# One condition per expert above 32 tokens, a later block of 64 rows, and a branch hint for PE in a mixture-of-experts kernel

## The chip, the cores and the metric

The kernel runs on one core of a Trainium2 chip. The metric is the device time of one execution in microseconds (us); lower is better. The engines are named as in the profile: PE (TensorE, matrix products and transposes; PEld its loads of stationary operands), DVE (VectorE), ACT (ScalarE), POOL (GpSimd), SP (SyncE, which here issues transfers). A q behind a name (PEq, PEldq, SPq) is that engine's sequencer or its DMA queue.

## The reference

One decoder layer in float32 on 512 tokens of width 1024: attention heads and recurrent heads, a projection and a layer norm, cross-attention and a layer norm, and a hierarchical mixture of experts with a last layer norm. The change touches only the experts:

```python
g_prob = softmax(xt @ w_group + b_group)            # 4 groups, the best one is taken
top_p, top_i = top_k(softmax(logits of the group), 2)   # 2 of its 8 experts
...
def run_block(xblk, e):
    hid = silu(xblk @ w_gate[e]) * (xblk @ w_up[e])     # 1024 -> 512
    return hid @ w_down[e]                              # 512 -> 1024
...
y = yb * slot_w
out = segment_sum(y, slot_tok)
```

512 tokens with two experts each give 1024 rows for 32 experts. For these inputs the experts 0 to 31 get 41, 41, 19, 5, 15, 74, 64, 9, 0, 4, 14, 1, 21, 11, 55, 28, 10, 92, 53, 14, 14, 133, 30, 162, 2, 19, 34, 6, 17, 11, 4 and 21 rows. Ten have more than 32 (0, 1, 5, 6, 14, 17, 18, 21, 23, 26), four of these more than 64 (5, 17, 21, 23).

## The kernel before

The experts are taken in order by a Python loop, so each has its own code. Expert e's first 64 rows stand in one half of a tile `xT` (two experts share one, turned by `turn_pair`), its weights in six tiles of 1 MB (`wg`, `wu`, `wd`, two each) in a ring of 20 places. SP fills the ring: `pump(2)` and `pump(4)` (line L815) issue the next two and four tiles of the list at their place in SP's program, and each issue waits until its place is free.

`step(now, last, M)` is one expert's work on PE: gate and up of this expert, and in between the transposes (`turn`, L1154) and the product with `wd` (`down`) of the expert before. Every `mm` is line L75. It exists twice, in two arms of a condition on n, the number of thresholds (32, 64, 192, 320, 448) that the expert's count exceeds: `If(n > 0)` at L1260 takes 64 rows, its Else 32 rows. Behind it `later_blocks` (L1198) has a condition of its own, `If(n > 1)`: `block128` takes up to 128 further rows, fetched into `xo` ahead of time, through transposes (L1122), gate into `psg`, up into `psu`, transposes (L1186) and `psy`; a loop inside `If(n > 2)` (L1201, L1202) repeats it. `send` scatters the rows of a pair of experts, `fetch` gathers rows; both are on POOL.

The order on PE, DVE, ACT and POOL is as written; each engine runs the conditions itself, with its own register loaded by `number(e)` (L1211). Order within the loop: `number`, `fetch`, every second time `turn_pair` and `fetch_pair`, the condition of `step`, `send`, `pump(2)`, the condition of `later_blocks`, `pump(4)`.

Of the kernel before, what the change touches and what calls it, by code (L numbers as in the profile page):

```python
# [964 lines left out]
def moe(ctx, tc, A, out, x2, x2d, env):  # L965
# [78 lines left out]
    steps = iota("steps", [5], [[P, 5]], 0, base=-64)  # L1044
    V.tensor_scalar(steps, steps, 32.0, None, op0=OP.max)
    nb = gp.tile([1, NE, 5], F32, name="nb")
    V.tensor_tensor(nb, cnt[0:1].unsqueeze(2).to_broadcast([1, NE, 5]), steps[0:1].unsqueeze(1).to_broadcast([1, NE, 5]), OP.is_gt)
# [49 lines left out]
    def bank(name, tag):  # L1097
        return banks.tile([P, 512], F32, name=name, tag=tag)
# [25 lines left out]

    class Expert:


        def __init__(self, e):
            self.e, self.c, self.r = e, e // 2, slice(e % 2 * 64, e % 2 * 64 + 64)
            self.x = xT[self.c]  # L1130
            if e % 2 == 0:
                Ys[self.c] = ms.tile([P, D], F32, name="Y", bufs=2)

        def gate_up(self, M, steps):

            e = self.e
            if steps[0] == 0:
                self.ps = bank("psgu", f"g{e % 2}")
            n = P // M // 2
            w = 512 // n  # L1140
            for k in steps:
                for q in range(2 * n):
                    mm(self.ps[q * M:q * M + M, 0:w], self.x[:, k, self.r.start:self.r.start + M],
                       W[e, "ug"[q // n], k // 4][:, k % 4, q % n * w:(q % n + 1) * w], k == 0, k == KD - 1)
            if steps[-1] == KD - 1:
                for q in range(n):
                    h = self.hs[0:M, q * w:(q + 1) * w]
                    SC.activation(h, self.ps[64 + q * M:64 + q * M + M, 0:w], AF.Silu)  # L1148
                    V.tensor_tensor(h, h, self.ps[q * M:q * M + M, 0:w], OP.mult)  # L1149

        def turn(self):
            pt = bank("psht", "h")
            for c in range(4):
                PE.transpose(pt[:, c * 64:(c + 1) * 64], self.hs[:, c // 2 * 256 + c % 2:(c // 2 + 1) * 256:2], ident[0:64, 0:64])  # L1154
            V.tensor_copy(self.hT, pt[:, 0:256])  # L1155

        def down(self):
            e = self.e
            ps = bank("psy", f"y{e % 2}")
            for c in range(4):  # L1160
                for q in range(2):
                    mm(ps[q * 64:q * 64 + 64, :], self.hT[:, c * 64:(c + 1) * 64],
                       W[e, "d", c // 2][:, c % 2, q * 512:q * 512 + 512], c == 0, c == 3)
            for q in range(2):
                SC.copy(Ys[self.c][self.r, q * 512:q * 512 + 512], ps[q * 64:q * 64 + 64, :])  # L1165

        def send(self):
            if self.e % 2:
                scatter(Ys[self.c], first_y[:, self.c:self.c + 1])

# [25 lines left out]
    def later_blocks(e, n, rows):  # L1196

        with tc.If(n > 1):  # L1198
            tiles = [ms.tile([P] + c, F32, name=t) for t, c in (("ox", [KD, P]), ("oh", [512]), ("oT", [512]))]
            block128(e, rows, tiles, later_y[:, 0, e:e + 1])  # L1200
            with tc.If(n > 2):  # L1201
                with tc.For_i(2, n) as c:  # L1202
                    c = nc.s_assert_within(c - 1, 1, 3, skip_runtime_bounds_check_because=FITS)
                    idx = ms.tile([P, 2], I32, name="oi")
                    for m, t in enumerate((later_x, later_y)):
                        V.tensor_copy(idx[:, m:m + 1], t[:, bass.ds(c, 1), e:e + 1].rearrange("p c e -> p (c e)"))
                    fetch(rows, idx[:, 0:1])
                    block128(e, rows, tiles, idx[:, 1:2])

    def number(e):  # L1210
        return nc.values_load(regs[0:1, e:e + 1], min_val=0, max_val=5, skip_runtime_bounds_check_because=FITS)  # L1211
# [26 lines left out]

    with tc.manual_schedule(engines={mybir.EngineType.PE, mybir.EngineType.DVE, mybir.EngineType.Activation, mybir.EngineType.Pool}):
# [7 lines left out]
        Expert.hs, Expert.hT = hs, hT  # L1247
# [3 lines left out]
        for e in range(NE):  # L1251
# [8 lines left out]
            with tc.If(n > 0) as many:  # L1260
                step(now, last, 64)
            with many.Else():
                step(now, last, 32)
            if last:
                last.send()
                pump(2)
            else:
                later_slots(marks)
                fetch(rows, later_x[:, 0, 0:1])
                cG.close()  # L1270
                env["cT"].close()
                env["more"](ctx, "ringC", RING_C)
            later_blocks(e, n, rows)
# [88 lines left out]
```

## Time and profile before

| | |
|---|---|
| three runs, median (lowest to highest) | 1177.45 us (1168.74 to 1178.84) |
| the profiled execution | 1178.46 us |
| its span, mean granted clock of TensorE | 1176.7 us, 0.931 |
| PE, PEld, DVE, ACT, POOL busy | 991.0, 649.1, 404.1, 312.6, 279.7 us |

The time is the device time of an execution; the span runs from the first to the last instruction in the trace of the profiled one. Busy shares are means over stages with different limits: the experts begin at about 584 us, half way, and before them the layer's other parts run. A group's row in the profile names line, engine, operation and tiles; where a row shows idle time, the name behind the arrow is what ended it.

### The profile page before, as it was taken

How to read it: one execution, taken by the hardware profiler on the slowest of the kernel's cores; microseconds unless marked ns; L12 is line 12 of the kernel's file. 1: busy time of each engine (PE TensorE's matmuls, PEld its weight loads, DVE VectorE, ACT ScalarE, POOL GpSimd, SP SyncE). 2: the span in 40 equal slices, each digit the busy share in tenths (PEclk: the TensorE clock that was granted, in tenths of full speed). 3: DMA queues.
4: the chain of work that ended last, by engine and by line, in shares of the span. 5: the costliest groups of instructions: out<-in, count | busy, mean ns of one | idle time of the engine just before them, and what ended most of it. 6: DMA issues, size and time to landing. Idle time of an engine off the chain costs nothing. (4 is left out here: it accounts for less than half of the span.)

```text
span 1176.7 us, 16302 instructions
## 1 busy us (share of the span) xinstructions
PE 991.0 (84%) x6260; PEld 649.1 (55%) x6260; DVE 404.1 (34%) x865; ACT 312.6 (27%) x612; POOL 279.7 (24%) x210
## 2 busy tenths in 40 slices
PE   7999999989899999999477997777897887877860
PEld 6787798768688998889223433332332333433320
DVE  8528607656835514345611101111100111011117
ACT  4434423433633534421011101111110101011132
POOL 4431243115124672331211101121101101011112
PEclk9999999999999999999688998898998899998885
DMA  6730231011043452178669959999999949299934
GB/s 206 218 105 24 56 101 37 1 36 55 20 143 93 141 163 71 54 264 332 265 263 413 413 210 397 414 411 414 413 417 400 403 183 407 98 412 412 411 109 180
DMA packets 88618, 269.59 MB, mean 229 GB/s; under 512 B 16191, under 2 KB 57212, under 8 KB 63870
## 3 DMA queue, kind: packets, MB, share of 16 engines
q1 hardware_dynamic: 76926, 252.67, 56.0%
q0 software_dynamic: 10512, 11.04, 2.8%
q10 hardware_dynamic: 1008, 3.67, 0.8%
q8 instruction: 98, 1.61, 0.6%
q14 instruction: 74, 0.61, 0.1%
HBM read 279.91 MB, written 14.68 MB: 250 GB/s over the span
## 5 line engine op out<-in xcount | busy, mean ns | idle before, releaser
L75 PE MATMUL psgu<-wu,xT 128*32 128x256 f32 (+1 forms) x864 | 190.9, 504 | 56.1 <-issue 32.2
L148 POOL TENSOR_TENSOR hl<-raw,hl 128x1024 fp32r<-128x1024 f32 (+1 forms) x67 | 161.4, 2411 | 252.9 <-ACT hl L145 201.9
L75 PE MATMUL psgu<-wg,xT 128*32 128x256 f32 (+1 forms) x864 | 192.8, 504 | 8.7 <-issue 8.7
L75 PEld LDWEIGHTS psgu<-wu,xT 128*32 128x32 f32 (+1 forms) x864 | 66.3, 134 | 151.5 <-issue 119.9
L75 PE MATMUL psy<-wd,hT 128*64 128x512 f32 x512 | 118.4, 600 | 0.7 <-ACTq L1198 0.6
L145 ACT CAST hl<-raw 128x1024 fp32r<-128x1024 f32 (+1 forms) x68 | 70.3, 1040 | 92.0 <-PE psm L75 39.0
L1114 POOL DMA_INDIRECT xo<-x2d,later_x x32 | 32.1, 1004 | 202.8 <-ACTq L1198 55.6
L1155 DVE COPY hT<-psht 128x256 f32<-128x256 f32 x32 | 13.6, 424 | 191.0 <-PE psht L1154 186.2
L1148 ACT ACTIVATE hs<-psgu 32x256 f32<-32x256 f32 (+1 forms) x54 | 22.6, 418 | 208.8 <-PE psgu L75 196.9
L75 PEld LDWEIGHTS psy<-wd,hT 128*64 128x64 f32 x512 | 35.3, 138 | 72.0 <-issue 70.2
L1149 DVE TENSOR_TENSOR hs<-hs,psgu 32x256 f32<-32x256 f32 (+1 forms) x54 | 24.8, 460 | 145.0 <-ACT hs L1148 82.5
L1165 ACT COPY Y<-psy 64x512 f32<-64x512 f32 x64 | 37.1, 580 | 135.2 <-PE psy L75 132.4
L75 PEld LDWEIGHTS psgu<-wg,xT 128*32 128x32 f32 (+1 forms) x864 | 66.8, 134 | 8.7 <-issue 8.4
L75 PE MATMUL psm<-hl,XO 128*128 128x256 f32 x384 | 50.7, 287 | 1.4 <-DVE x L680 1.4
L1122 PE MATMUL psgt<-ident,xr 128*128 128x128 f32 x128 | 22.6, 323 | 33.5 <-PEq L1198 21.2
L75 PE MATMUL psm<-hl,mix 128*128 128x256 f32 x320 | 49.1, 291 | 0.6 <-DVE x L680 0.5
L1106 POOL DMA_INDIRECT yd<-Y,first_y x16 | 16.1, 1009 | 139.4 <-ACTq L1198 125.8
L75 PEld LDWEIGHTS psm<-hl,XO 128*128 128x128 f32 x384 | 47.3, 191 | 2.1 <-DVE x L680 1.8
L75 PE MATMUL psxq<-x1T,hl 128*128 128x512 f32 x192 | 46.7, 396 | 0.0
L75 PEld LDWEIGHTS psm<-hl,mix 128*128 128x128 f32 x320 | 43.5, 193 | 3.5 <-issue 1.3
L75 PE MATMUL psq<-xT,hl 128*128 128x512 f32 x192 | 45.2, 395 | 0.0
L1122 PEld LDWEIGHTS psgt<-ident,xr 128*128 128x128 f32 x128 | 18.5, 212 | 46.2 <-issue 28.9
(368 smaller groups left out, 1669.4 us busy)
## 6 DMA issues: line engine op xcount, KB each, us to landing
wg<-in_moe_w_gate_dram SPq DMA_DIRECT2D x64, 1024.0 KB
wu<-in_moe_w_up_dram SPq DMA_DIRECT2D x64, 1024.0 KB
wd<-in_moe_w_down_dram SPq DMA_DIRECT2D x64, 1024.0 KB
raw<-in_w_in_dram SPq DMA_DIRECT2D x22, 512.0 KB
raw<-in_w_out_dram SPq DMA_DIRECT2D x8, 512.0 KB
raw<-in_xa_wv_dram SPq DMA_DIRECT2D x8, 512.0 KB
raw<-in_xa_wk_dram SPq DMA_DIRECT2D x8, 512.0 KB
raw<-in_xa_wq_dram SPq DMA_DIRECT2D x8, 512.0 KB
```

Source lines behind the costliest of these rows:

```text
L75: PE.matmul(o, l, r, start=start, stop=stop, skip_group_check=True)
L145: cp = SC.copy(hl[:, 0], raw)
L148: (V if n - look < on_dve else PO).tensor_tensor(hl[:, 1], raw, f(hl[:, 0]), OP.subtract)
L1106: t = PO.indirect_dma_start(out=yd, out_offset=bass.IndirectOffsetOnAxis(ap=idx, axis=0), in_=Y, in_offset=None, bounds_check=2 * S - 1, o ...
L1114: PO.indirect_dma_start(out=rows, out_offset=None, in_=x2d, in_offset=bass.IndirectOffsetOnAxis(ap=idx, axis=0), bounds_check=S - 1, oob_i ...
L1122: PE.transpose(ps[:, k * P:(k + 1) * P], rows[:, a * 512 + k:(a + 1) * 512:4], ident)
L1148: SC.activation(h, self.ps[64 + q * M:64 + q * M + M, 0:w], AF.Silu)
L1149: V.tensor_tensor(h, h, self.ps[q * M:q * M + M, 0:w], OP.mult)
L1155: V.tensor_copy(self.hT, pt[:, 0:256])
L1165: SC.copy(Ys[self.c][self.r, q * 512:q * 512 + 512], ps[q * 64:q * 64 + 64, :])
```

## The change

The thresholds become 128, 32, 64, 192, 320 and 448. For every expert but the first there is one condition, `If(n > 0, label="more{e}")`. Its arm holds the 64-row `step` and, nested, the later blocks: `If(n > 1)`, in it `If(n > 2)` with `block128` and its loop (now `n > 3`), and in that one's Else the new `block64`, for up to 64 further rows in the form of the 64-row arm. Its Else is the 32-row `step`. `send`, `pump(2)` and `pump(4)` stand behind the condition. Both arms begin with `hint(e + 1)`: an instruction on PE that names the next expert's condition and says that its branch, to the Else, is likely taken.

```diff
-    steps = iota("steps", [5], [[P, 5]], 0, base=-64)
-    V.tensor_scalar(steps, steps, 32.0, None, op0=OP.max)
-    nb = gp.tile([1, NE, 5], F32, name="nb")
-    V.tensor_tensor(nb, cnt[0:1].unsqueeze(2).to_broadcast([1, NE, 5]), steps[0:1].unsqueeze(1).to_broadcast([1, NE, 5]), OP.is_gt)
+    steps = iota("steps", [6], [[P, 6]], 0, base=-192)
+    V.memset(steps[:, 0:1], 128.0)
+    V.memset(steps[:, 1:2], 32.0)
+    nb = gp.tile([1, NE, 6], F32, name="nb")
+    V.tensor_tensor(nb, cnt[0:1].unsqueeze(2).to_broadcast([1, NE, 6]), steps[0:1].unsqueeze(1).to_broadcast([1, NE, 6]), OP.is_gt)
...
+    def gate_up(ps, x, e, steps, M=64):
+
+        n = P // M // 2
+        w = 512 // n
+        for k in steps:
+            for q in range(2 * n):
+                mm(ps[q * M:q * M + M, 0:w], x[:, k, 0:M],
+                   W[e, "ug"[q // n], k // 4][:, k % 4, q % n * w:(q % n + 1) * w], k == 0, k == KD - 1)
...
+    def block64(e, rows, tiles, idx):
+
+        xe, hs, hT = tiles[0][:, :, 0:64], tiles[1][0:64], tiles[2][:, 0:256]
+        tags = "o", f"y{e % 2}"
+        for a in range(2):
+            ps = bank("psgt", tags[a])
+            for k in range(4):
+                PE.transpose(ps[:, k * 64:(k + 1) * 64], rows[0:64, a * 512 + k:(a + 1) * 512:4], ident[0:64, 0:64])
+            (SC.copy if a else V.tensor_copy)(xe[:, 4 * a:4 * a + 4, :], ps[:, 0:256].rearrange("p (k t) -> p k t", t=64))
+        ps = bank("psg", "o")
+        gate_up(ps, xe, e, range(KD))
+        hidden(ps, hs)
+        turn(hs, hT)
+        down(bank("psy", tags[1]), hT, e, rows[0:64])
+        scatter(rows, idx)
...
     def later_blocks(e, n, rows):
 
+        def tiles():
+            return [ms.tile([P] + c, F32, name=t) for t, c in (("ox", [KD, P]), ("oh", [512]), ("oT", [512]))]
+
         with tc.If(n > 1):
-            tiles = [ms.tile([P] + c, F32, name=t) for t, c in (("ox", [KD, P]), ("oh", [512]), ("oT", [512]))]
-            block128(e, rows, tiles, later_y[:, 0, e:e + 1])
-            with tc.If(n > 2):
-                with tc.For_i(2, n) as c:
-                    c = nc.s_assert_within(c - 1, 1, 3, skip_runtime_bounds_check_because=FITS)
-                    idx = ms.tile([P, 2], I32, name="oi")
-                    for m, t in enumerate((later_x, later_y)):
-                        V.tensor_copy(idx[:, m:m + 1], t[:, bass.ds(c, 1), e:e + 1].rearrange("p c e -> p (c e)"))
-                    fetch(rows, idx[:, 0:1])
-                    block128(e, rows, tiles, idx[:, 1:2])
+            with tc.If(n > 2) as more:
+                ts = tiles()
+                block128(e, rows, ts, later_y[:, 0, e:e + 1])
+                with tc.If(n > 3):
+                    with tc.For_i(3, n) as c:
+                        c = nc.s_assert_within(c - 2, 1, 3, skip_runtime_bounds_check_because=FITS)
+                        idx = ms.tile([P, 2], I32, name="oi")
+                        for m, t in enumerate((later_x, later_y)):
+                            V.tensor_copy(idx[:, m:m + 1], t[:, bass.ds(c, 1), e:e + 1].rearrange("p c e -> p (c e)"))
+                        fetch(rows, idx[:, 0:1])
+                        block128(e, rows, ts, idx[:, 1:2])
+            with more.Else():
+                block64(e, rows, tiles(), later_y[:, 0, e:e + 1])
...
+    def hint(e):
+        if e < NE:
+            tc.mark_branch_hint_location(f"more{e}", "LikelyTaken", engines=[mybir.EngineType.PE])
...
-            with tc.If(n > 0) as many:
-                step(now, last, 64)
-            with many.Else():
-                step(now, last, 32)
-            if last:
-                last.send()
-                pump(2)
-            else:
+            if e == 0:
+                with tc.If(n > 0) as many:
+                    step(now, last, 64)
+                with many.Else():
+                    step(now, last, 32)
                 later_slots(marks)
                 fetch(rows, later_x[:, 0, 0:1])
                 cG.close()
                 env["cT"].close()
                 env["more"](ctx, "ringC", RING_C)
-            later_blocks(e, n, rows)
+                hint(1)
+                later_blocks(e, n, rows)
+            else:
+                with tc.If(n > 0, label=f"more{e}") as many:
+                    hint(e + 1)
+                    step(now, last, 64)
+                    later_blocks(e, n, rows)
+                with many.Else():
+                    hint(e + 1)
+                    step(now, last, 32)
+                last.send()
+                pump(2)
             pump(4)
             last = now
 
```

The functions `gate_up`, `hidden`, `turn` and `down` hold what the methods of `Expert` held; `block64` uses them for `rows[0:64]`, with gate and up in one bank `psg`.

How the program stands on PE. Before, from the end of expert 1's 32-row arm to the loop behind its later block (names: `psy` is a product with `wd`, `xo` the later rows, `ox`, `oh` and `oT` the block's copies):

```order
L75 MATMUL psgu<-wg,xT 32x256 x2
L75 MATMUL psy<-wd,hT 64x512 x8
L1260 UNCONDITIONAL_BRANCH
L1198 COMPARE_AND_BRANCH
L1122 MATMUL psgt<-ident,xo 128x128 x8
L75 MATMUL psg<-wg,ox 128x512 x8
L75 MATMUL psu<-wu,ox 128x512 x8
L1186 MATMUL psht<-ident,oh 128x128 x4
L75 MATMUL psy<-wd,oT 128x512 x8
L1201 COMPARE_AND_BRANCH
L1202 COMPARE_AND_BRANCH
L1202 UNCONDITIONAL_BRANCH x2
```

The two arms of the step join here, and only then comes the condition of the later block. In the changed program, the end of expert 2's 64-row arm: both new conditions and the block of 128 follow it directly:

```order
L75 MATMUL psgu<-wg,xT 64x512
L1229 COMPARE_AND_BRANCH
L1230 COMPARE_AND_BRANCH
L1123 MATMUL psgt<-ident,xo 128x128 x8
L75 MATMUL psg<-wg,ox 128x512 x8
L75 MATMUL psu<-wu,ox 128x512 x8
L1214 MATMUL psht<-ident,oh 128x128 x4
L75 MATMUL psy<-wd,oT 128x512 x8
L1233 COMPARE_AND_BRANCH
L1234 COMPARE_AND_BRANCH
```

The later block has moved into the arm, ahead of the small one. Further on in expert 2, from the last rows of the block of 64 into the small arm:

```order
L1146 MATMUL psht<-ident,oh 128x64 x4
L75 MATMUL psy<-wd,oT 64x512 x8
L1230 UNCONDITIONAL_BRANCH
L1229 UNCONDITIONAL_BRANCH
L1396 BRANCH_PREFETCH_HINT
L75 MATMUL psgu<-wu,xT 32x256 x2
L75 MATMUL psgu<-wg,xT 32x256 x2
L75 MATMUL psgu<-wu,xT 32x256 x2
```

Two unconditional branches now lie between a later block and the next expert, and the small arm begins with a hint. From its end to expert 3, still on PE:

```order
L75 MATMUL psy<-wd,hT 64x512 x8
L1310 UNCONDITIONAL_BRANCH
L1245 TENSOR_LOAD regs
L1310 COMPARE_AND_BRANCH
L1396 BRANCH_PREFETCH_HINT
L75 MATMUL psgu<-wu,xT 64x512
L75 MATMUL psgu<-wg,xT 64x512
```

The small arm stood next to the 64-row arm, 108 instructions behind its condition and followed by the condition of the later blocks; it now stands behind both forms of the later block, 507 instructions behind the one condition, and nothing follows it but the jump to the next expert. (A listed f32 matmul counts as four instructions, a transpose as two.) From the end of a 64-row arm without later block the way is one jump of 397 and one of 175; from the end of a block of 128 it is about 300 and 176. The first hint, `hint(1)`, stands as the second row of PE's whole program.

On SP, which issues the weights. Before, from the end of an early expert's step to its later blocks:

```order
L1260 UNCONDITIONAL_BRANCH x2
L815 DMA wd<-in_moe_w_down_dram 128x2048
L815 DMA wg<-in_moe_w_gate_dram 128x2048
L815 DMA wu<-in_moe_w_up_dram 128x2048
L1198 COMPARE_AND_BRANCH
L1201 COMPARE_AND_BRANCH
L1202 COMPARE_AND_BRANCH
```

Some issues stand ahead of the later blocks here. In the changed program, from the end of an early expert's condition:

```order
L1233 UNCONDITIONAL_BRANCH
L1230 UNCONDITIONAL_BRANCH
L1229 UNCONDITIONAL_BRANCH
L1310 UNCONDITIONAL_BRANCH
L815 DMA wg<-in_moe_w_gate_dram 128x2048
L815 DMA wu<-in_moe_w_up_dram 128x2048
L815 DMA wd<-in_moe_w_down_dram 128x2048 x2
L815 DMA wg<-in_moe_w_gate_dram 128x2048
L815 DMA wu<-in_moe_w_up_dram 128x2048
```

The two issues of `pump(2)` (and what the scheduler had left over from the expert before) stood ahead of the condition of the later blocks; now all stand behind the one condition, and SP passes the branches of the later blocks only inside its arm.

## Rows read from the trace of the kernel before

**Rows 1.** The page: busy time by engine, GB/s in 40 slices, the queue of instructions.

```profile
...
PE 991.0 (84%) x6260; PEld 649.1 (55%) x6260; DVE 404.1 (34%) x865; ACT 312.6 (27%) x612; POOL 279.7 (24%) x210
...
GB/s 206 218 105 24 56 101 37 1 36 55 20 143 93 141 163 71 54 264 332 265 263 413 413 210 397 414 411 414 413 417 400 403 183 407 98 412 412 411 109 180
...
q8 instruction: 98, 1.61, 0.6%
...
```

**Rows 2.** Three stretches: us, five engines' busy time, PEclk, DMA share, GB/s.

```profile
...
683.90:695.10 11.20, 9.42 (x22) 3.96 (x23) 1.38 (x2) 0.59 (x1) 0.00 (x0) 0.85 0.00 0
957.20:970.30 13.10, 10.29 (x26) 4.27 (x24) 2.07 (x3) 0.59 (x1) 0.00 (x0) 1.00 0.04 5
1005.60:1026.20 20.60, 17.84 (x44) 7.65 (x42) 2.07 (x3) 1.18 (x2) 0.00 (x0) 1.00 0.00 1
...
```

**Rows 3.** Waits, 590 to 1135 us: in total, times, longest.

```profile
...
PEld psgu L75 <- DMA wu<-in_moe_w_up_dram: 11.6, 5, 3.6
...
PE psgt L1122 <- PEq L1198: 21.2, 14, 4.4
...
```

**Rows 4.** The same columns for four experts, 17, 22, the last eight, behind.

```profile
...
740.20:790.50 50.30, 40.40 (x355) 17.98 (x355) 6.06 (x14) 8.25 (x17) 6.70 (x7) 0.90 1.02 413
848.30:886.10 37.80, 34.29 (x115) 14.37 (x114) 4.05 (x7) 4.11 (x7) 1.69 (x2) 1.00 1.00 411
970.30:980.00 9.70, 9.14 (x94) 4.54 (x94) 1.63 (x4) 1.91 (x4) 1.01 (x1) 1.00 0.96 377
1026.40:1123.00 96.60, 72.75 (x584) 30.89 (x583) 10.81 (x24) 15.01 (x30) 14.07 (x14) 0.87 0.99 402
1123.00:1138.50 15.50, 14.63 (x107) 6.22 (x108) 1.67 (x4) 2.79 (x6) 1.01 (x1) 0.91 0.05 13
...
```

**Rows 5.** DMA queues, five experts from 740.2 to 803.9: packets, MB, share.

```profile
...
q8 instruction: 10, 0.16, 1.1%
...
```

**Rows 6.** Lines L1198, L1260, L1201 on PE's sequencer: ns min/median/max.

```profile
...
L1198 PEldq COMPARE_BRANCH  x32: 78/1673/6134, 593.3 to 1128.8; - x32
...
L1198 PEldq EVENT_SEMAPHORE  x28: 51/51/51, 594.0 to 1132.4; - x28
...
L1260 PEldq COMPARE_BRANCH  x42: 70/232/5657, 583.8 to 1121.0; - x42
...
L1201 PEldq COMPARE_BRANCH  x8: 174/204/356, 685.3 to 1025.3; - x8
...
```

**Rows 7.** Timeline of PE at expert 2: start, length, idle before and releaser.

```profile
...
615.26 0.64 PE L75 MATMUL psgu<-wu,xT 128*32 128x256 f32 x2 [5.08 <-PEq L1198]
...
```

**Rows 8.** Timeline of PE in expert 5.

```profile
...
659.77 3.60 PE L75 MATMUL psy<-wd,hT 128*64 128x512 f32 x16
663.20 0.59 PE L75 MATMUL psgu<-wu,xT 128*64 128x512 f32 x1
...
663.63 0.59 PE L75 MATMUL psgu<-wu,xT 128*64 128x512 f32 x1
...
666.73 1.23 PE L1122 MATMUL psgt<-ident,xo 128*128 128x128 f32 x8
668.81 7.13 PE L75 MATMUL psg<-wg,ox 128*128 128x512 f32 x16 [0.85 <-DVE ox L1123]
675.78 7.03 PE L75 MATMUL psu<-wu,ox 128*128 128x512 f32 x16
...
685.24 8.80 PE L75 MATMUL psy<-wd,oT 128*128 128x512 f32 x16 [0.83 <-issue]
694.99 0.64 PE L75 MATMUL psgu<-wu,xT 128*64 128x512 f32 x1 [0.95 <-PEq L1201]
...
```

**Rows 9.** Timeline of SP's queue in expert 5: weight issues.

```profile
...
666.84 0.33 SPq L815 DMA_DIRECT2D wu<-in_moe_w_up_dram  x1
694.16 0.33 SPq L815 DMA_DIRECT2D wg<-in_moe_w_gate_dram  x1
...
```

More of the change, by code (lines that the diff above doesn't have):

```diff
@@ L1123, in turned, with hidden, turn, down @@
             copies[a](xT[:, 4 * a:4 * a + 4, :], ps.rearrange("p (k t) -> p k t", t=P))
+    def gate_up(ps, x, e, steps, M=64):
[5 more added lines that the diff above has]
+                   W[e, "ug"[q // n], k // 4][:, k % 4, q % n * w:(q % n + 1) * w], k == 0, k == KD - 1)
+    def hidden(ps, hs, M=64):
+        n = P // M // 2
+        w = 512 // n
+        for q in range(n):
+            h = hs[0:M, q * w:(q + 1) * w]
+            SC.activation(h, ps[64 + q * M:64 + q * M + M, 0:w], AF.Silu)
+            V.tensor_tensor(h, h, ps[q * M:q * M + M, 0:w], OP.mult)
+    def turn(hs, hT):
+        pt = bank("psht", "h")
+        for c in range(4):
+            PE.transpose(pt[:, c * 64:(c + 1) * 64], hs[:, c // 2 * 256 + c % 2:(c // 2 + 1) * 256:2], ident[0:64, 0:64])
+        V.tensor_copy(hT, pt[:, 0:256])
+    def down(ps, hT, e, Y):
+        for c in range(4):
+            for q in range(2):
+                mm(ps[q * 64:q * 64 + 64, :], hT[:, c * 64:(c + 1) * 64],
+                   W[e, "d", c // 2][:, c % 2, q * 512:q * 512 + 512], c == 0, c == 3)
+        for q in range(2):
+            SC.copy(Y[:, q * 512:q * 512 + 512], ps[q * 64:q * 64 + 64, :])
     class Expert:
@@ L1129, in __init__ @@
             self.e, self.c, self.r = e, e // 2, slice(e % 2 * 64, e % 2 * 64 + 64)
-            self.x = xT[self.c]
+            self.x = xT[self.c][:, :, self.r]
             if e % 2 == 0:
@@ L1134, in gate_up @@
         def gate_up(self, M, steps):
-            e = self.e
             if steps[0] == 0:
[L1138 to L1144, printed above, removed]
+                self.ps = bank("psgu", f"g{self.e % 2}")
+            gate_up(self.ps, self.x, self.e, steps, M)
             if steps[-1] == KD - 1:
[L1146 to L1149, printed above, removed]
+                hidden(self.ps, hs, M)
         def turn(self):
[L1152 to L1155, printed above, removed]
+            turn(hs, hT)
         def down(self):
[L1158 to L1165, printed above, removed]
+            down(bank("psy", f"y{self.e % 2}"), hT, self.e, Ys[self.c][self.r])
         def send(self):
@@ L1169, in send @@
                 scatter(Ys[self.c], first_y[:, self.c:self.c + 1])
+    def block64(e, rows, tiles, idx):
[9 more added lines that the diff above has]
+        hidden(ps, hs)
+        turn(hs, hT)
+        down(bank("psy", tags[1]), hT, e, rows[0:64])
+        scatter(rows, idx)
     def block128(e, rows, tiles, idx):
@@ L1246, in moe @@
             PO.memset(t, 0.0)
-        Expert.hs, Expert.hT = hs, hT
         turn_pair(0)
```

2 lines of the change are left out of this document (1 added, 1 removed).

## The prediction

> **What bounds the kernel now.** I read the page first. PE is busy 84% of the span, but the DMA row of the last 17 slices is near 410 GB/s with three holes [rows 1], so the question is which of the two, PE or the stream of expert weights, sets the end in the expert loop (from 583.8 us, the first branch of L1260 on PE [rows 6], to the end). Stretches of time answer that. While PE works on the later blocks of experts 5, 21 and 23, the weights stand still for 11.2, 13.1 and 20.6 us at 0, 5 and 1 GB/s [rows 2]: all 20 places are full and PE is late. PE waited for weights only 11.6 us in five places [rows 3]; by expert these lie between 13 and 17, where the ring has run empty. So up to expert 17 the weights decide, and from there on PE alone: every microsecond that PE gains or loses after 848.3 moves the end until a hole is used up.
>
> Next, what PE does in an ordinary expert. From 740.2 to 790.5 are four experts of at most 32 tokens, 12.6 us each, though PE is busy 40.4 us in them, 10.1 each; expert 22, for which nothing was late, took 9.7 us at full clock [rows 4]. The difference is the sequencer. PE's instructions come in packets of their own, 98 of 16 KB in 1.61 MB [rows 1]. The built program has 25,161 PE instructions (a listed f32 matmul is two weight loads and two matmuls), so a packet is a block of 256. In the five experts from 740.2 to 803.9, ten came, one per 6.4 us [rows 5]: two per expert, at a steady beat. Branches show the wait: that of L1198 takes between 0.08 and 6.13 us with a median of 1.67, that of L1260 up to 5.66; behind L1198 PE's transposes alone lost 21.2 us in 14 places [rows 3], and after such a branch expert 2 began 5.08 us late [rows 6, 7].
>
> **Part by part.** The sum is made on the profiled execution, 1178.46 us (span 1176.7); the median is 1.0 below.
>
> *Block of 64 (experts 5 and 17; 74 and 92 tokens).* From 666.73 to the end of the last product at 685.24 + 8.80 = 694.04 the block takes 27.3 us [rows 8]. Its gate and up are 7.13 + 7.03 us and become the form of the 64-row arm, one group each 0.43 us apart (16 of them, 6.9); its product with wd falls from 8.80 to the 3.60 of that arm; transposes, copies and silu stay about 4.4. Together 14.9, so PE gains 12.4. Expert 17's stretch ran at clock 1.00 [rows 4], where 16 such matmuls take 7.0 instead of 8.8, so its block is 1.8 shorter to begin with and I take -10.5. For expert 5 the gain goes through the weights: the hole of 11.2 us closes only in part, because the change also moves two issues. SP issues two tiles at 665 and 666.84, ahead of the block, and four at 694.16 behind it [rows 9]; now all six stand behind the branch. A tile takes 2.6 us (1 MiB at 402 GB/s), so the stream dries up 5.3 us earlier, at 678.6, and starts again at about 682.7: a hole of 4.1, a gain of 7. PE gives some of its 12.4 back in the experts between. I take **-6** at expert 17's start (bounds -11 and +2) and **-10.5** for 17 itself (-12.4 to -4.5, if a block of instructions has to be fetched in it).
>
> *The same two tiles at 21 and 23.* The stream dries up 5.3 us sooner there too, and it has two more tiles to bring after 1026. There the weights run at 0.99 of the DMA engines until about 1123 [rows 4], while expert 31 ends after that; I count **0** (to +5), but the cover is thin: it caps what the last eight experts can gain at about 6 us.
>
> *Jumps of experts with at most 32 tokens (ten behind expert 17: 19, 20, 22, 24, 25, 27 to 31).* Before, they jump 108 instructions to their arm and 274 over the later block: always into the block being read or the next one, and every block is fetched, two and a bit per expert. Now they jump once, over 507: never into the next block, but only the blocks that are executed are needed. They execute some 190 instructions, 1.74 blocks on average; at 6.4 us that is 11.1 against 12.6, a gain of 1.6 if the hinted fetch takes the place of the useless one exactly. No trace here shows a hint for a forward branch, so the price is bounded: -2.9 (the 9.7 of expert 22) to +4 (a fetch of 6, two of them behind PE's queued work). The nearest row is the steady beat of fetches; I take half the gain, -0.7, also because the waiting semaphore at each skipped branch (28 of them) falls away [rows 6]: **-7**.
>
> *Jumps of experts with 33 to 64 tokens (18 and 26).* They had +172 and +274, and now +397 over all later blocks and at once +175 over the other arm: 126 instructions farther, half a block, and the hint has pointed the other way. A block costs 6.4; half is 3.2, and a wrong hint costs something: **+4** each, bounds 0 and +9.
>
> *Behind the block of 128 (21 and 23; 133 and 162 tokens).* PE's branch at L1201 now takes 0.17 to 0.36 us, in shadow [rows 6], as it lands in a block that came during the long products. Now two jumps follow each other, about +300 over the block of 64 and +176 over the small arm, 476 in all with PE empty: most starts end two blocks on, a fetch of 6 that nothing hides. **+6** each, bounds 0 and +12.
>
> *Other edits* cost nothing visible: one column more in a table that is made before 585, a hint per arm, register tables, and for GpSimd the scatter of Y now behind the later block, whose rows nobody reads before the end.
>
> Sum: -6 - 10.5 + 0 - 7 + 8 + 12 = -3.5, so 1175.0; less 1.0 to the median, **1174 us**.
>
> **A rule beside this.** The row first: a PE branch took up to 6.13 us and the packets are of 16 KB [rows 1, 6]. The Trainium skill ("Runtime: NRT & Kernel Launch", Instruction fetch mechanics) says that an engine holds two such pages, that the prefetch is purely sequential, and that a taken branch out of them waits for a DMA fetch. The trace agrees as to block and wait. It speaks against this change, which makes each ordinary jump longer than a page, and names no hint; by it the time would be the 1225 of the third rival below. The same section says that fetching is hidden behind the pace of issue; here the trace differs: 12.6 us per expert with 10.1 of work [rows 4].
>
> **Rivals.** *The hint hides the jump fully* and the jumps behind 18, 21, 23 and 26 find their block. Then ordinary experts come down to expert 22's 9.7 until the weights stop them: 19, 20 and 22 give -2.2 each, the last eight -6 together (the cap above), 5 gives -7, 17 gives -10.5, the rest nothing: -30, **1148**; with a third of the far jumps still paid, 1154. For it: expert 22 shows that 9.7 is possible. Against it: the fetches already come back to back, and one cannot be early if its predecessor is late.
>
> *The far jumps each pay twice* (slower). The 64-row experts and those with later blocks are hinted wrongly, since the hint always favours the small arm: the next block in sequence has then not been fetched when PE runs into it, and the jump out of the arm pays again. 12 instead of 4 at 18 and 26, 18 instead of 6 at 21 and 23, +6 at 17: 46 more, of which the parts under 27-us blocks are hidden, about half: **1198**. It decides from four fetches not hidden. For it: 5.08 us after a single late branch [rows 7]. Against it: in a block of 27 us there is time for four fetches.
>
> *The hint does nothing, or comes too late* (slower; the change doesn't do what it says). Each of the ten ordinary experts behind 17 pays the rest of a fetch, +4, so +40 in place of -7, and those before 17 fall below the weights' pace and lose expert 5's gain: +47 + 7 - 3.5 = +50, **1225**. For it: no hint was seen to act in this trace, and 507 is always out of the next block. Against it: the hint is given 13 us ahead, twice the beat.
>
> **How the numbers follow.** Forecast 0.37 (what a measurement can tell from no change is about 1%, 1166 to 1189), full hiding 0.31, paying twice 0.17, no hint 0.15. So faster 0.31, same 0.37, slower 0.32. The forecast's own range is 1164 to 1188; to hold 8 in 10 the range reaches to 1147 for the first rival and to 1212 for the second, and leaves out the third and the tails.
>
> **What the profile after would show.** Right: psgu and psy of the 64-row form in the later blocks of 5 and 17, some 15 us long; the hole at 684 about 4 us; ordinary experts 11 to 13 us apart; fewer instruction packets per expert than two; PE branches at the new conditions short for ordinary experts and near 6 us for 18, 21, 23 and 26. The first rival: ordinary experts below 10.5 us apart and the weights at 1.0 of the DMA engines through 1123. The second: branches of 6 us in pairs. The third: the branch of nearly every ordinary expert at 4 to 6 us. I am wrong in sum if the hint fails, or if the weights' two late tiles matter at 31.

## The result and the profile after

Ten runs of the changed kernel have a median of 1160.53 us (1157.79 to 1166.7), ten of the kernel before 1178.05 us; the ratio is 0.9868, 95% interval 0.984 to 0.9896. It is faster by 1.3%, some 15.5 us by the ratio. The forecast of 1174 us, "same", was too slow; the time lies inside its range and between the forecast and the first rival. The profiled execution took 1160.54 us with a span of 1157.2, 19.5 less than the span before.

From the page of the changed kernel, against [rows 1]: PE's busy time, GB/s in 40 slices, the queue of PE's instructions.

```profile
...
PE 969.1 (84%) x6260; PEld 640.3 (55%) x6260; DVE 401.6 (35%) x864; ACT 313.4 (27%) x614; POOL 279.7 (24%) x210
...
GB/s 210 215 113 19 56 92 55 1 37 25 50 111 126 125 168 73 55 206 359 288 159 371 394 326 414 415 413 413 413 419 415 417 316 379 56 410 414 414 201 178
...
q8 instruction: 96, 1.57, 0.5%
...
```

The three holes in the weights have become one deep one (slice 35) and some notches. The program has 29,160 PE instructions in place of 25,161, yet 96 packets of them came, not 98.

Stretches of the changed kernel, with the columns of [rows 4] (us, busy time of five engines, PEclk, DMA share, GB/s): expert 17, expert 18, 22, 23, the hole in 23, and experts 24 to 30.

```profile
...
840.80:867.00 26.20, 23.67 (x114) 8.80 (x116) 2.54 (x5) 2.72 (x5) 2.50 (x3) 1.00 1.02 419
867.00:880.40 13.40, 12.45 (x66) 4.85 (x63) 1.21 (x3) 2.96 (x6) 2.02 (x2) 1.00 1.02 417
951.30:967.40 16.10, 12.45 (x92) 5.53 (x92) 1.60 (x4) 1.76 (x4) 1.01 (x1) 0.68 0.93 365
967.40:1013.00 45.60, 35.97 (x117) 15.09 (x119) 4.20 (x7) 4.27 (x8) 4.04 (x4) 0.96 0.47 178
985.20:1008.50 23.30, 20.53 (x50) 8.84 (x48) 2.07 (x3) 1.18 (x2) 0.00 (x0) 0.99 0.01 1
1013.00:1106.00 93.00, 71.54 (x584) 31.71 (x587) 10.79 (x24) 15.00 (x30) 13.06 (x13) 0.87 1.01 413
...
```

Expert 17 takes 26.2 us where it took 37.8 [rows 4], expert 18 takes 13.4 (19.0 before, as the starts of PE's gate and up show), expert 22 takes 16.1 where it took 9.7. The block of 64 itself, in PE's timeline of expert 5 (start, length, idle before and releaser):

```profile
...
669.57 1.14 PE L1190 MATMUL psgt<-ident,xo 64*128 64x64 f32 x8 [1.00 <-DMA xo<-x2d,later_x]
...
681.00 0.69 PE L1146 MATMUL psht<-ident,oh 64*128 64x64 f32 x4 [1.41 <-DVE oh L1141]
682.21 3.65 PE L75 MATMUL psy<-wd,oT 128*64 128x512 f32 x16 [0.52 <-DVE oT L1147]
685.69 0.59 PE L75 MATMUL psgu<-wu,xT 128*64 128x512 f32 x1
...
```

It runs from 669.57 to 685.86, 16.3 us against 27.3 before [rows 8].

The same view behind expert 21's block of 128 and behind expert 23's:

```profile
...
943.66 2.31 PE L75 MATMUL psy<-wd,oT 128*128 128x512 f32 x5
951.26 0.61 PE L75 MATMUL psgu<-wu,xT 128*32 128x256 f32 x2 [5.29 <-issue]
...
956.74 0.58 PE L75 MATMUL psgu<-wu,xT 128*32 128x256 f32 x1 [3.65 <-issue]
...
980.81 1.23 PE L1123 MATMUL psgt<-ident,xo 128*128 128x128 f32 x8 [2.10 <-DMA xo<-x2d,later_x]
...
1000.30 7.11 PE L75 MATMUL psy<-wd,oT 128*128 128x512 f32 x16 [0.83 <-issue]
1012.96 0.64 PE L75 MATMUL psgu<-wu,xT 128*32 128x256 f32 x2 [5.55 <-issue]
...
```

PE stands for 5.29 and 5.55 us before the next expert begins, and expert 22 begins at a lower clock (0.68 in the stretch above, 1.00 before [rows 4]) and stops once more for 3.65 us. Against that, the wait for the later rows `xo` in expert 23 is 2.10 us, and was 7.06. And the branches on PE's sequencer, ns min/median/max: L1310, the one condition of each expert, and L1229, that of the later blocks (L1198 in the kernel before).

```profile
...
L1310 PEldq COMPARE_BRANCH  x31: 74/4191/6296, 597.4 to 1099.8; - x31
...
```

```profile
...
L1229 PEldq COMPARE_BRANCH  x15: 73/458/3656, 593.0 to 1046.8; - x15
...
```

The median wait of the one condition is 4.19 us, longer than that of either condition before [rows 6]: the hint did not hide the jump. Of the 22 experts with at most 32 rows, where this branch is taken, 18 wait more than 3 us at it. As there is one such branch in place of two, all of PE's branches in the experts still sum to 123 us instead of 135. It still has to be said what the hint does.

Behind the two blocks of 128 the wait stands at this condition too. The first view shows L1233, by which PE leaves the block, the second the one condition from 944 to 1014, that is of experts 22, 23 and 24:

```profile
...
L1233 PEldq COMPARE_BRANCH  x4: 245/345/404, 937.3 to 1007.6; - x4
...
```

```profile
...
L1310 PEldq COMPARE_BRANCH  x3: 83/4058/4227, 946.9 to 1008.5; - x3
...
```

The way out of the block takes 0.40 us at most, and it is one jump to the next expert's condition: no branch of L1229 stands between them in the trace, so the second jump of 176, over the small arm, that the section on the change names is not run here. The jump of 507 into the small arm of experts 22 and 24 takes 4.06 and 4.23 us, with PE empty.

### The profile page after: what moved, and what is told of

It is laid out like the page before. It is cut to its first block, busy times and chain, and to the rows that moved or that the text cites. A ratio compares the mean times of both kernels' runs of the same rounds, so it can differ in the third digit from the quotient of the medians.

```text
span 1157.2 us, 16066 instructions
## 1 busy us (share of the span) xinstructions
PE 969.1 (84%) x6260; PEld 640.3 (55%) x6260; DVE 401.6 (35%) x864; ACT 313.4 (27%) x614; POOL 279.7 (24%) x210
## 5 line engine op out<-in xcount | busy, mean ns | idle before, releaser
L75 PEld LDWEIGHTS psgu<-wu,xT 128*32 128x32 f32 (+1 forms) x864 | 69.6, 132 | 166.4 <-issue 147.0
L75 PEld LDWEIGHTS psgu<-wg,xT 128*32 128x32 f32 (+1 forms) x864 | 65.7, 132 | 12.1 <-issue 11.2
L414 DVE TENSOR_REDUCE st<-pss 128x1 f32<-128x128 f32 (+1 forms) x64 | 30.5, 486 | 35.3 <-PE pss L75 34.0
L75 PEld LDWEIGHTS psq<-xT,hl 128*128 128x128 f32 x192 | 36.0, 188 | 8.9 <-issue 0.2
```

Source lines behind the costliest of these rows:

```text
L75: PE.matmul(o, l, r, start=start, stop=stop, skip_group_check=True)
L414: V.tensor_reduce(st[:, 0, i:i + 1], ps[:, 0:n], AX.X, OP.max, negate=True)
```

## The experiments

All ratios are to the kernel before, run on the same chip, with 95% intervals. A difference in us between two runs is that of their medians; the runs are from different chips, and by the ratios such a difference comes out up to 6 us smaller or 2 larger. L1310, L1311 and L1313 are the one condition per expert, as the kernels' lines move.

### Is the gain that of the block of 64 alone?

The loop of the kernel before, with the changed `later_blocks` and thresholds:

```diff
-            else:
-                with tc.If(n > 0, label=f"more{e}") as many:
-                    hint(e + 1)
-                    step(now, last, 64)
-                    later_blocks(e, n, rows)
...
+            with tc.If(n > 0) as many:
+                step(now, last, 64)
+            with many.Else():
+                step(now, last, 32)
...
+            later_blocks(e, n, rows)
```

> The kernel before with nothing but the block of 64 for experts 5 and 17 (two conditions per expert stay, no hint, the two early weight issues stay ahead of the later block). Theory A, the two shorter blocks are the whole gain and the new branches are worth nothing: 1160 us, within 4 of the changed kernel. Theory B, the single condition and its hint carry part of it: 1167 to 1172 us.

Measured 1208.79 us, ratio 1.0247 (1.0193 to 1.0302): slower by 2.5%. Both theories fall. The block of 64 gains on PE (expert 17 takes 30.1 us, expert 5 28.6, where they took 37.8 and 39.5), and most of the others lose. The branch over the later blocks, ns min/median/max:

```profile
...
L1229 PEldq COMPARE_BRANCH  x32: 78/4891/7922, 595.0 to 1159.2; - x32
...
```

Its median is 4.89 us, where the same branch had 1.67 before [rows 6]. Four experts from 742.6 to 809.6 took 67.0 us, and eleven instruction packets came in them (this view is that of [rows 5]):

```profile
...
q8 instruction: 11, 0.18, 1.1%
...
```

That is 2.75 packets per expert, one per 6.1 us, where it had been two per expert, one per 6.4 us [rows 5]. An expert's code is 680 to 695 PE instructions now and was 557 to 572.

### Does the rest help without the block of 64?

The changed kernel, with `later_blocks` of block 128 alone:

```diff
-            with tc.If(n > 2) as more:
-                ts = tiles()
-                block128(e, rows, ts, later_y[:, 0, e:e + 1])
+            ts = tiles()
+            block128(e, rows, ts, later_y[:, 0, e:e + 1])
...
-            with more.Else():
-                block64(e, rows, tiles(), later_y[:, 0, e:e + 1])
```

> The changed kernel without the block of 64: experts 5 and 17 run the block of 128 again; one condition, hints and the moved issues stay. Theory A: 1176 to 1184 us, no better than before. Theory B: 1165 to 1172 us, as the condition and the hint keep their share.

Measured 1177.51 us, ratio 0.9972 (0.9945 to 1.0): no change, as theory A says. So neither part is worth anything alone: the block of 64 costs 2.5%, the condition and hint bring nothing, and together they bring 1.3%.

### Does the hint act?

Every hint names expert 31's condition, so that no instruction moves:

```diff
-            tc.mark_branch_hint_location(f"more{e}", "LikelyTaken", engines=[mybir.EngineType.PE])
+            tc.mark_branch_hint_location(f"more{NE - 1}", "LikelyTaken", engines=[mybir.EngineType.PE])
```

> The changed kernel with every hint naming expert 31's condition, so that the program keeps its length and addresses and only the last hint is of use. Theory A, the hint acts on a few branches only (those of experts 4, 19, 20 and 30 took 0.5 to 1.2 us, most others 4 to 6): those few go to 4 to 6 us, the others do not move, 1160 to 1172 us. Theory B, the hint carries the change: every branch of an ordinary expert goes to 6 us or more, over 1180 us. Theory C, the hint does nothing at all: the same branches within 0.3 us and the same time within 3 us.

Measured 1220.8 us, ratio 1.0332 (1.0276 to 1.0388): the hints are worth 60 us (55 by the ratios). Theory B is right in sign and size. Its reason holds in part: all 22 branches that are taken now wait 3.4 us or more, but the median rises only from 4.19 to 5.64 us.

```profile
...
L1310 PEldq COMPARE_BRANCH  x31: 77/5643/7414, 602.2 to 1162.3; - x31
...
```

```profile
...
q8 instruction: 12, 0.20, 1.0%
...
```

```profile
...
q8 instruction: 10, 0.16, 1.1%
...
```

The last two fences are the instruction packets in experts 8 to 12, without hints (78.8 us) and with them (62.3 us): twelve and ten. The whole run had 111 packets, against 96. So with the right hints fewer blocks are fetched for the same work; which ones are saved the counts do not say. Most of the 60 us stands in PE's branches: those at the one condition sum to 127.0 us instead of 101.3, those at L1229 to 41.1 instead of 16.9. A hint that names a far branch might cost something by itself, and no run has this program with no hint at all; the last experiment, whose kernel has none on one side, comes to 44 us.

### Are the moved weight issues free?

In the kernel before, `pump(2)` behind the later block, nothing else:

```diff
                 last.send()
-                pump(2)
...
-            pump(4)
+            pump(6 if last else 4)
```

> The kernel before with pump(2) moved behind the later block, six issues together, and nothing else. Theory A (the forecast's step): the stream runs dry some 5 us sooner in the later blocks of 5, 21 and 23, but PE sets the end there: same as before within 5 us, holes of 16 to 26 us in place of 11 to 21. Rival: the weights set the end behind expert 23 and the two late tiles show, 5 to 10 us slower.

Measured 1180.44 us, ratio 0.9989 (0.9957 to 1.0022): no change. But the run does not test the step. SP's issues are placed by the scheduler, and it put them where they were: built, this program has the same instructions in the same order on every engine as the kernel before. SP's queue in expert 5, whose later block begins on PE at 668.12:

```profile
...
666.51 0.33 SPq L815 DMA_DIRECT2D wg<-in_moe_w_gate_dram  x1
668.23 0.33 SPq L815 DMA_DIRECT2D wu<-in_moe_w_up_dram  x1
693.85 0.33 SPq L815 DMA_DIRECT2D wg<-in_moe_w_gate_dram  x1
...
```

Two issues still stand ahead of the block, as in [rows 9], and the holes are 10.5, 14.8 and 20.3 us where they were 11.2, 13.1 and 20.6 [rows 2]. What the moved issues cost by themselves stays open. The run is of use as a second profile of one program: single experts differ by up to 1.7 us between the two, the start of expert 17 by 2.2.

### Is it the length of the code?

The two-condition kernel of the first experiment without the loop for experts of more than 192 rows, 151 PE instructions per expert:

```diff
-                with tc.If(n > 3):
-                    with tc.For_i(3, n) as c:
...
-                        fetch(rows, idx[:, 0:1])
-                        block128(e, rows, ts, idx[:, 1:2])
```

> The two-condition kernel with the block of 64, and the loop for experts of more than 192 rows left out (no expert here has so many; for other inputs part of the work would be missing). Its code per expert falls by some 140 PE instructions. Theory D, an expert costs as many instruction blocks as its code touches, at 6 us each, and the block of 64 was slow alone only by its length: ordinary experts back to about 12 us, the two shorter blocks stay, 1155 to 1165 us. Rival, the second nested condition with its joins is what cost the 29 us: 1195 to 1210 us, as with the loop.

Measured 1137.62 us, ratio 0.9673 (0.9632 to 0.9714), 71 us faster than with the loop, though not one instruction of the loop is ever run. Theory D holds in sign; the gain is larger than it said. The code is now also shorter than that of the kernel before (529 to 544 instructions). The branch:

```profile
...
L1229 PEldq COMPARE_BRANCH  x32: 78/2130/6200, 599.7 to 1094.6; - x32
...
```

With PE faster the weights stand still less: the holes in expert 23 are 3.5 and 9.2 us, where the same kernel with the loop has one of 22.1. Both issue two tiles ahead of the block, so that is not the reason. The cut takes the loop out of the other engines' programs too; their branches at L1229 have medians of about 0.05 us in both runs, so the wait that it shortens is PE's.

The same cut in the changed kernel:

> The changed kernel without the loop for more than 192 rows (no expert here has so many; for other inputs part of the work would be missing): the ordinary experts' jump falls from 507 to some 370 instructions. Theory D with hints: what is jumped over and hinted is not fetched, so its length is worth little here, unlike the 71 us that the same cut gave with two conditions: 1150 to 1163 us. Rival, the length costs here too, half a block for each of 22 ordinary experts: 1125 to 1140 us.

Measured 1146.68 us (1139.29 to 1152.78), ratio 0.9735 (0.9675 to 0.9795): some 14 us faster than with the loop, between the two expectations. With hints the length costs about a fifth of what it costs without. Both short kernels leave out work that other inputs need.

### What do hints on branches that fall through cost?

The ten experts with more than 32 rows get no hint of their own (it names expert 31's condition, as above):

```diff
-            tc.mark_branch_hint_location(f"more{e}", "LikelyTaken", engines=[mybir.EngineType.PE])
+            tc.mark_branch_hint_location(f"more{NE - 1 if e in {0, 1, 5, 6, 14, 17, 18, 21, 23, 26} else e}", "LikelyTaken", engines=[mybir.EngineType.PE])
```

> The changed kernel with the hints for the ten experts of more than 32 rows turned to expert 31's condition, so that a branch that falls through is not hinted; addresses unchanged. Theory F, a wrong hint costs the next block in sequence: experts 5, 6, 14, 17, 18, 21, 23 and 26 start up 2 to 6 us faster, 1150 to 1158 us. Rival, wrong hints cost nothing since PE's queued work covers them: 1158 to 1164 us.

Measured 1177.27 us, ratio 0.9993 (0.9961 to 1.0026): the wrong hints are worth 17 us (15 by the ratios), and theory F has the wrong sign. The count of packets says nothing here, 97 against 96; the branches at L1229 sum to 39.8 us instead of 16.9. Expert 18 shows how. The first fence is the changed kernel, the second this one: L1229, which jumps over the later blocks and then over the small arm; the third is PE's timeline here.

```profile
...
L1229 PEldq COMPARE_BRANCH  x2: 208/333/458, 873.8 to 878.4; - x2
...
```

```profile
...
L1229 PEldq COMPARE_BRANCH  x2: 209/3294/6379, 887.0 to 893.5; - x2
...
```

```profile
...
894.17 1.20 PE L1123 MATMUL psgt<-ident,xr 128*128 128x128 f32 x8 [2.78 <-PEq L1229]
899.35 0.64 PE L75 MATMUL psgu<-wu,xT 128*32 128x256 f32 x2 [3.98 <-issue]
...
```

The jump of 397 took 0.46 us with the hint for expert 18's own condition and 6.38 without. It lands two instructions ahead of the small arm (the fences on PE in the section on the change show the place). So the block that the hint brings for an arm that is not taken is here the block in which the taken arm comes out. Of the five experts with 33 to 64 rows that have a hint, three show it: at 1, 14 and 18 the jump takes 0.38 to 0.48 us with the hint and 6.03 to 6.38 without. At 6 and 26 it takes the same in both (0.36 and 0.34, 2.55 and 2.83).

### When must the hint be given?

The hint moved from the heads of both arms to just ahead of the condition before it:

```diff
+                hint(e + 1)
                 with tc.If(n > 0, label=f"more{e}") as many:
-                    hint(e + 1)
                     step(now, last, 64)
                     later_blocks(e, n, rows)
                 with many.Else():
-                    hint(e + 1)
                     step(now, last, 32)
```

> The changed kernel with the hint for the next expert moved from the head of both arms to just ahead of this expert's condition. Theory E, a hint acts when PE's sequencer enters the block that holds the hinted branch, so given at the arm's head it comes too late whenever arm and branch share a block: those branches (about half of the ordinary experts) lose up to 6 us, 1145 to 1157 us. Rival, a hint that replaces the one before it just ahead of its branch undoes that one: as without hints, over 1200 us.

Measured 1150.15 us (1149.44 to 1151.19), ratio 0.9784 (0.9742 to 0.9826). The branch's median falls from 4.19 to 0.71 us:

```profile
...
L1311 PEldq COMPARE_BRANCH  x31: 73/708/6399, 598.2 to 1085.3; - x31
...
```

This fits theory E: one or two instructions earlier, ahead of the jump into the arm instead of behind it, the hint is in time more often (9 of the 22 taken branches wait more than 3 us, in place of 18). That jump itself can take 6 us; whether the place of the hint counts or those 6 us is not separated. A new hint just ahead of the old one's branch does not undo the old one.

### Arm and branch in one block

As above, and the end of the large arm filled so that the small arm begins a block of 256 instructions:

```diff
+                    nc.tensor.addr_align(256, offset=255, max_nops=0)
                 with many.Else():
```

> As the kernel with the early hint, and the 32-row arm put at the start of a block of 256 instructions, so that arm and next branch lie in one block. Theory E: one fetch of 6 us per ordinary expert, hidden under 8 to 9 us of work: ordinary experts 9 to 10.5 us apart, branches under 1 us, and the weights set the end: 1135 to 1150 us. Rival, the fetch cannot start before the branch: 12 us apart, 1160 us or more.

Measured 1155.27 us, ratio 0.9823 (0.9781 to 0.9865): worse than the early hint alone. Ordinary experts reach the 9 us that was expected (3, 4, 8, 9 and 10 take 9.0 to 9.1), but experts 6, 14 and 18 take 22.4 to 23.5, as their way out now lies in the block ahead of the arm, which no hint brings: in all five experts with 33 to 64 rows this jump takes 5.85 to 6.09 us. So the filling was moved inside the condition of the later blocks, which puts the way out in the arm's block:

```diff
             with more.Else():
                 block64(e, rows, tiles(), later_y[:, 0, e:e + 1])
+            if e:
+                nc.tensor.addr_align(256, offset=24, max_nops=0)
```

> The complete kernel with the early hint, and aligned so that the place where the 64-row arm lands behind the later blocks, the 32-row arm and the next branch lie in one block. Theory G, the hint on a 64-row expert is useful though its branch falls through, because it fetches the block in which that expert's way out lands (with it 0.46 us at expert 18's way out, without it 6.38): here way out, arm and branch need one fetch: ordinary experts 9 us, 64-row experts 13 to 15 us, 1135 to 1147 us. Rival, alignment brings the 64-row experts nothing: as the first aligned kernel, 1150 to 1158 us.

Measured 1149.79 us (1147.78 to 1152.22), ratio 0.9768 (0.9736 to 0.98). The one condition, ns, and three stretches (experts 8 and 9, experts 11 to 13, and the hole in expert 23):

```profile
...
L1313 PEldq COMPARE_BRANCH  x31: 73/359/5987, 600.0 to 1084.0; - x31
...
```

```profile
...
704.00:722.00 18.00, 16.95 (x176) 7.85 (x169) 3.18 (x7) 5.35 (x11) 4.00 (x4) 1.00 1.02 412
739.00:787.00 48.00, 28.27 (x260) 13.01 (x257) 4.43 (x10) 6.33 (x13) 6.56 (x7) 0.89 1.02 416
979.50:1000.80 21.30, 18.55 (x45) 7.88 (x44) 2.07 (x3) 1.18 (x2) 0.00 (x0) 1.00 0.00 0
...
```

The branch's median is 0.36 us and experts 8 and 9 (704 to 722) take 9.1 and 9.6 us. Yet the kernel gains nothing on the one with the early hint: from 739 on the weights run at 416 GB/s and the three experts take 16 us each, the pace of six tiles. What PE gains there it waits for weights. The expectation of 9 us held only ahead of that; 64-row experts came to 22.8 (expert 6), 15.9 (14), 20.7 (18) and 13.2 (26). Their way out takes 0.43 and 0.45 us at 14 and 26, and 6.01 and 6.07 at 6 and 18, so theory G is shown at 14 and 26 and not at 6 and 18, which follow a later block.

### The place in the block

64 transposes, 128 instructions, in the loop of expert 0, which is never run:

```diff
                         block128(e, rows, ts, idx[:, 1:2])
+                        if e == 0:
+                            ps = bank("psgt", "o")
+                            for k in range(64):
+                                PE.transpose(ps[:, 0:P], ident, ident)
```

> The changed kernel with 64 transposes, 128 PE instructions or half a block, in a loop of expert 0 that is never run: all later experts start half a block further on. Theory E: which branches are late depends on where they fall in a block, so the set changes from expert to expert (branches of 0.5 us become 4 to 6 us and the reverse) while the sum over 31 experts stays within some 10 us: 1152 to 1172 us. Rival, the place in the block is of no account: the same branches are short, 1158 to 1163 us.

Measured 1154.86 us (1153.53 to 1159.68), ratio 0.9815 (0.9777 to 0.9854): 6 us from the changed kernel, for instructions that nobody runs; the intervals of the two overlap. The branches of experts 19, 20 and 30 went from 0.92, 0.59 and 1.23 us to 5.54, 5.97 and 6.12, those of 28 and 31 from 6.03 to 0.47 and 0.46. So the set of late branches changes, as theory E says; their sum falls from 101 to 87 us, a little more than it allowed. Expert 18 takes 22.0 us here and expert 26 13.5, where the changed kernel has 13.4 and 21.3: which of the two is short is a matter of place.

### The hint without the single condition

The first experiment's kernel, complete, with one hint per expert that names the condition of the later blocks:

```diff
+            if e:
+                tc.mark_branch_hint_location(f"later{e}", "LikelyTaken", engines=[mybir.EngineType.PE])
             with tc.If(n > 0) as many:
                 step(now, last, 64)
```

> The complete two-condition kernel with the block of 64 and its loop, which alone took 1209 us, and one thing more: a hint per expert, given just ahead of the condition of the step, that names the condition of the later blocks as likely jumped over. The single condition is not in it, and two weight issues stay ahead of the later block. Theory H, the hint is what pays for the block of 64, and the single condition is of no account: the jump over the later blocks no longer waits for a useless block, ordinary experts at 12 to 13 us, the hole of the weights in expert 23 some 5 us smaller than in the changed kernel: 1138 to 1155 us. Rival, the single condition is needed, since the code of both arms and the join are still read: 1175 to 1205 us.

Measured 1164.85 us (1160.2 to 1168.22), ratio 0.9889 (0.9862 to 0.9915): 44 us better than without the hint and 10 above what theory H gave. The hint pays for the block of 64 in this form too. The single condition matters less: without useful hints it costs 12 us (1220.8 against 1208.79); with them it gains 4, which the intervals do not tell from nothing (the changed kernel), or 15 (the one with the early hint, which like this one gives its hint ahead of the condition of the step). The branch, and the packets over the whole run:

```profile
...
L1229 PEldq COMPARE_BRANCH  x32: 83/2656/6193, 597.5 to 1113.0; - x32
...
```

```profile
...
q8 instruction: 97, 1.59, 0.6%
...
```

97 packets, against 113 without the hint.

## Why the prediction came out as it did

The time lies in the range, and the sum was near. The steps under it fared unequally, here on the profiled executions (starts of each expert's gate and up on PE):

- **Block of 64.** Expert 17's start: -7.5 us where -6 was said; the hole at 682 is 3.0 us where 4.1 was said. Expert 17 itself: -11.6, said -10.5. Right, with the mechanism, and the cap by the weights at expert 5 as well; with the block of 128 in its place, and the rest of the change kept, expert 17 starts 3.1 us later than before.
- **The two moved tiles**: said 0 (to +5). No run has them moved and nothing else, so this term is not shown. The hole in expert 23 is 23.3 us against 20.6 before [rows 2]; experts 24 to 30 then run at 413 GB/s throughout, so the cover was thin there, as the step feared.
- **Ordinary experts.** 19, 20, 25 and 27 to 31 together gave -7.6 us (with what follows 31), said -0.7 each, -5.6. Right in size, but not by the mechanism. The hinted fetch did not take the place of the useless one: two packets per expert still came (ten in experts 8 to 12), and most of the jumps wait 4 to 6 us. And -7.6 is the difference of larger terms that the step did not see apart: the same program takes 60 us more without useful hints, some 43 of them (1220.8 against 1177.27) by the hints of the experts with at most 32 rows. The third rival's price for a hint that does nothing, 1225 us (its own terms give 1228), was met by the run with dummy hints, 1221. The first rival counts -2.2 us at expert 22, which took the 9.7 us already.
- **Jumps of 64-row experts.** This is the step that failed in sign. Said: +4 each at 18 and 26, because the jump is longer "and the hint has pointed the other way". Measured: -5.6 and +2.6. At 18 the hint points to the block in which the expert comes out; without such hints the ten experts above 32 rows cost 17 us. The second rival's premise, that these hints hurt, fell with it. That it is 18 and not 26 that gained is a matter of place: with the code half a block further on, the two together give -2.1, not far from the -3.0 here.
- **Behind the block of 128.** Said +6 each, for two jumps out of the block. At 21 +5.8, and at 22, which follows, +6.5 more, since behind 5.29 us of idle PE the clock was lower and PE stood again (3.65). At 23 -0.9 and at 24 -1.2; PE stood 5.55 us there too, but the wait for `xo` fell from 7.06 us to 2.10. Together +10.2, for +10.6 said with the -0.7 of 22 and of 24. The place was right, the cause was not: the way out takes 0.40 us at most, and PE waits 4.06 and 4.23 us at the next ordinary expert's own jump. That the sum fits is luck.

These sum to -19.5, against -3.5 said. 11 of the 16 us between them are the 64-row experts, 2.6 the block of 64, the rest small.

Of the signs that the profile was to show, the form and length of the block of 64 (16.3 us), the hole at 684 (3.0) and ordinary experts some 12 us apart in the mean came. Three did not: the packets per expert stayed at two; the branches were not short for ordinary experts, 18 of 22 over 3 us, which was the sign of the third rival; and they were not near 6 us at 18, 21 and 23 (0.46 us at most), only partly at 26 (2.55 and 3.66). So the prediction had the stretches right and the waits of PE's sequencer largely wrong.

The rule of the Trainium skill that was set against the change ("Runtime: NRT & Kernel Launch", Instruction fetch mechanics: a taken branch out of the two pages held waits for a DMA fetch) is borne out by the branch of 6.38 us without a hint and of 0.46 with it. What it says of prefetch, that it is purely sequential, does not hold where a hint is armed: 111 packets with dummy hints became 96, and 113 without any became 97 with one per expert in the last experiment.

What stays open: why the ordinary experts' packets come 6 us apart in these stretches; what the moved weight issues cost; and whether the short kernel without hints (1137.62 us) is faster than the short one with them (1146.68), as their intervals overlap. The fastest complete kernels are the one with the early hint and the second aligned one, 1150 us each.

## What to carry to other kernels

Code that is jumped over is not free on PE when work per branch is short: 151 instructions per expert that never ran cost 71 us over 32 experts without hints and 14 with them, and a special case that saves some 11 us twice in the changed kernel made the kernel slower by 2.5% until a hint paid for its length. So price an added arm by the instruction blocks that every pass must read past it, and look in the trace at the packets per pass and at the waits of the branches. The count alone does not give the time: 96 and 97 packets went with 1160.5 and 1177.3 us, 92 and 79 with 1150. A hint is worth giving ahead of the jump into its block, and it can be of use by the block that it brings even where its branch is not taken, as at three of five experts here.

## What the runs showed of the hardware that was not expected

- In stretches of ordinary experts PE's instruction packets come one per 6.1 us in the first experiment (11 in 67.0 us), 6.2 in the changed kernel (10 in 62.3), 6.6 with dummy hints (12 in 78.8) and 6.4 before. These are means; with the arms aligned to blocks the whole run needs only 79.
- A branch hint that names a branch which falls through still moves the fetch: 0.46 against 6.38 us for the later jump at expert 18, and likewise at two of the four other experts of 33 to 64 rows with a hint.
- A hint did more ahead of the jump into the arm than just behind it, at the arm's head: the median wait of the hinted branch was 0.71 us against 4.19.
- After 5.29 us in which PE stood, the mean granted clock in expert 22 was 0.68, a good part of it at the lower of the two levels (1.2 and 2.4 GHz), where the same expert had 1.00 before. After 5.55 us, in expert 24 (1013.0 to 1026.1), it was 0.88, and 0.99 before.
